# Low halves of the weight pieces of an encoder layer: a ScalarE copy with the sign turned and an accumulating DMA from GpSimd, where VectorE subtracted

## The chip, the cores and the metric

One core of a Trainium2 chip runs the whole kernel. The metric is device time in microseconds (us) of one execution, and the median of the runs is what is compared. A profile of one execution gives the trace; its span runs from the first to the last instruction, and the execution's own time is a little longer.

## The reference, cut to what matters

One layer of an encoder is applied to two request groups with the same weights: a prompt of 512 positions and a sample of 1024, both 1024 wide.

```python
h = _ln(x) * (1.0 + scale1) + shift1
proj = jnp.einsum('bld,de->ble', h, w_in)            # 1024 -> 4608
a = silu(_ln(_dwconv(a_val * sigmoid(a_gate))))      # 31 taps along positions
y_a = jnp.einsum('blc,cd->bld', a, conv_pw_w)
zb = x1 * _fftconv(v, filt[:, 0], hy_skip[0])        # long convolutions by FFT
zb = x2 * _fftconv(zb, filt[:, 1], hy_skip[1])
y_b = jnp.einsum('blc,cd->bld', zb, hy_out_w)
m = jax.nn.sigmoid(g_a) * y_a + jax.nn.sigmoid(g_b) * y_b
x = _ln(DEEPNORM_ALPHA * x + gate1 * (m @ w_out), ln1_g, ln1_b)
h = _ln(x) * (1.0 + scale2) + shift2
f = jnp.square(jax.nn.relu(h @ mlp_w1 + mlp_b1))     # 1024 -> 4096
x = _ln(DEEPNORM_ALPHA * x + gate2 * (f @ mlp_w2 + mlp_b2), ln2_g, ln2_b)
```

All of it is float32. The filters of the long convolutions come from a small MLP on the positions.

## The kernel before

A float32 product is made of three TensorE products of a shorter type, float32r: each operand is split into a high part (the value rounded to float32r) and a low part (the value minus its high part), and `mm3` adds high x high, high x low and low x high in PSUM. Activations are split where they are made. Weights come in **pieces** of 128 x 512 floats, 256 KB, 520 in all, and `wpiece_` makes each: SyncE's queue loads it into a `raw` buffer (4 of them); in 24 pieces near the end of each MLP VectorE multiplies a gate into `raw`; ScalarE copies `raw` to the high half of a `wt` buffer, which rounds it; VectorE subtracts that high half from `raw` into the low half. There are 6 `wt` buffers of two halves; 9 of the 520 pieces go into another pool, `pg`. `wpiece` raises the priority of these instructions.

The **main line** of work is, for the prompt group and the sample group in turn: `w_in` (72 pieces for each group, two at a time), `branches` (`w_y`, two at a time), `w_out_ln1` (four pieces serve a quarter of the columns), and `mlp`. The MLP runs in units of four hidden blocks. A unit multiplies the four hidden blocks with the left half of the columns of `mlp_w2` (four pieces, called phase D here), then with the right half (four other pieces, phase E); between units `mlp_up` makes the next hidden blocks with two pieces of `mlp_w1` each, the first of them before D. In D and E each of the four pieces is read in every block of 128 rows, so that all four are let go in the last block of the phase.

The **side line** is what the main line doesn't need at once: the filter MLP, the filters and their spectra (PSUM tiles `fx`), the 31-tap convolution (tiles `cv`, VectorE alone), the Hyena convolutions (FFT by matmuls). `pump` weaves it into the main line: a meter adds up an estimated cost of VectorE's and of TensorE's instructions, and side steps are taken while VectorE's sum is behind TensorE's. Each call of `self.V` is charged; calls through `self.nc.scalar` and `self.nc.gpsimd` are not.

The framework then orders each engine's instructions once more by priority and by its own estimate of when each is ready. Each engine executes its instructions in that order, and an instruction that waits holds all behind it on its engine. GpSimd (POOL) has little to do before: it clears tiles (`fp`, `cv`, `sg`) and issues the DMAs of the filter MLP's positions (`in_z_*`, 10 partitions, 40 KB, L617). Every VectorE instruction that goes through the meter, and every matmul, is shown at line L142.

Of the kernel before, what the change touches and what calls it, by code (L numbers as in the profile page):

```python
# [14 lines left out]
AF = mybir.ActivationFunctionType  # L15
ALU = mybir.AluOpType
# [142 lines left out]
class Enc:  # L159
# [50 lines left out]
    def wpiece_(self, src, shape, gate=None, w=None):  # L210
        raw = self.p_raw.tile(list(shape), F32, tag="raw", name="raw")
        self.nc.sync.dma_start(raw, src)
        if gate is not None:
            self.V.tensor_tensor(raw, raw, gate, op=ALU.mult)
        if w is None:
            w = self.p_wt.tile([128, 2] + list(shape[1:]), F32R, tag="wt", name="wt")
        self.split(raw, w[:, 0], w[:, 1])
        return w

    def mm3(self, ps, ah, al, bh, bl, first, last):  # L220
# [1159 lines left out]
```

## Time and profile before

| | us |
|---|---|
| median of 3 runs (2404.87 to 2413.45) | 2409.81 |
| the profiled execution | 2409.17 |
| its span | 2407.4 |
| TensorE (PE) busy in the span | 2339.7 |
| VectorE (DVE) busy | 1715.6 |
| ScalarE (ACT) busy | 859.7 |
| GpSimd (POOL) busy | 54.3 |

The profile page counts busy time by engine and shows it in 40 equal slices of the span. Other views list groups of equal instructions, who waited for whom, busy time in chosen stretches, the chain of work that ended last, and the instructions in order of time. Matmuls overlap, so that the mean duration of one is longer than its share of busy time.

### The profile page before, as it was taken

Reading aid. Unit: us, or ns where it says so; the run is one execution under the profiler, and the core shown is the slowest. Engines: PE = TensorE matmul, PEld = TensorE weight load, DVE = VectorE, ACT = ScalarE, POOL = GpSimd, SP = SyncE. Lnnn points to the kernel's source line nnn. Section 1 sums busy time; section 2 is a strip of 40 time slices with the busy share of each in tenths; the row PEclk is TensorE's granted clock in tenths of the full one; section 3 lists DMA queues with packets and bytes.
Section 4 is the critical chain, followed back from the end, with each engine's and each line's share of the span. In section 5 each row is a group of like instructions: output and inputs, shape, how many; then the busy total and the mean of one; then the engine's idle time right before and its main releaser. Section 6 shows DMA issues by size and latency. Waiting matters only on the chain.

```text
span 2407.4 us, 32989 instructions
## 1 busy us (share of the span) xinstructions
PE 2339.7 (97%) x12032; PEld 1947.7 (81%) x12032; DVE 1715.6 (71%) x3397; ACT 859.7 (36%) x1451; POOL 54.3 (2%) x149
## 2 busy tenths in 40 slices
PE   6999999999999999899999999999999999999997
PEld 3878777888888888888888887899888888888786
DVE  5988797877999989877988858749823433234567
ACT  3364422422222223465443352224742322322231
POOL 2110100000000000000000000000000000000000
PEclk9999999999999999999999999999999999999999
DMA  6555425663464566634433255544421111112231
GB/s 240 182 170 171 145 93 196 205 218 127 166 208 162 187 225 216 199 107 126 144 103 119 83 183 177 179 136 145 141 79 45 60 45 43 53 53 84 83 97 70
DMA packets 157864, 328.89 MB, mean 137 GB/s; under 512 B 18777, under 2 KB 27147, under 8 KB 157189
## 3 DMA queue, kind: packets, MB, share of 16 engines
q1 hardware_dynamic: 156869, 325.76, 41.1%
q8 instruction: 95, 1.56, 0.3%
q0 software_dynamic: 832, 1.02, 0.2%
q14 instruction: 68, 0.56, 0.1%
HBM read 265.04 MB, written 61.66 MB: 136 GB/s over the span
## 4 chain that ended last, share of the span: by engine, by line
PE 63%; DVE 9%; DMA 4%; issue 2%; ACT 1%; SPq 0%; DVEq 0%; ACTq 0%
PE mm L142 53%; PE fx L142 9%; DVE pg L142 3%; DVE fp L142 1%; DVE wt L142 1%; DMA sg<-ks 1%; PE tr L142 1%; DVE st L142 1%; DVE sg L142 1%; DVE sm L142 1%; DMA fp<-in_dec_s_dram 1%; DVE cv L142 1%; DMA pg<-d_grow 0%; DMA raw<-in_mlp_w_dram 0%; DMA sg<-in_ffn_w_dram 0%
## 5 line engine op out<-in xcount | busy, mean ns | idle before, releaser
L142 PE MATMUL mm<-pg,wt 128*128 128x512 f32 (+1 forms) x5544 | 1308.3, 391 | 4.1 <-DVE pg L142 3.3
L142 PEld LDWEIGHTS mm<-pg,wt 128*128 128x128 f32 x5544 | 1024.2, 189 | 219.5 <-issue 15.6
L142 PE MATMUL mm<-wt,pg 128*128 128x512 f32 (+1 forms) x3264 | 642.0, 355 | 7.2 <-DVE wt L142 3.8
L142 PEld LDWEIGHTS mm<-wt,pg 128*128 128x128 f32 x3264 | 537.3, 190 | 92.7 <-DVE wt L142 5.0
L199 ACT ACTIVATE wt<-raw 128x512 fp32r<-128x512 f32 x511 | 320.3, 630 | 743.7 <-PE mm L142 608.7
L142 DVE TENSOR_TENSOR wt<-raw,wt 128x512 fp32r<-128x512 f32 x511 | 346.3, 687 | 177.5 <-ACT wt L199 175.6
L142 DVE SCALAR_TENSOR_TENSOR cv<-cv,pp 128x512 f32<-128x512 f32 (+1 forms) x288 | 289.3, 1012 | 7.0 <-ACT cv L850 2.4
L142 DVE TENSOR_TENSOR pg<-so,pg 128x512 fp32r<-128x512 f32 (+1 forms) x219 | 135.4, 623 | 166.4 <-ACT so L1008 134.1
L142 DVE TENSOR_TENSOR pg<-pg,mm 128x512 f32<-128x512 f32 x168 | 113.6, 684 | 154.4 <-PE mm L142 154.3
L142 PEld LDWEIGHTS fx<-fp,fft 128*128 128x128 f32 x1536 | 177.5, 192 | 20.9 <-issue 14.2
L142 PE MATMUL fx<-fp,fft 128*128 128x128 f32 x1536 | 184.2, 277 | 2.1 <-DVE fp L142 1.0
L142 DVE TENSOR_TENSOR fp<-fp 128x256 f32<-128x256 f32 (+2 forms) x328 | 145.4, 483 | 16.2 <-ACT fp L377 10.8
L142 DVE TENSOR_TENSOR sg<-fx,sg 128x512 f32<-128x512 f32 (+1 forms) x162 | 98.8, 631 | 43.8 <-PE fx L142 29.5
L1006 ACT ACTIVATE so<-mm,pp 128x512 f32<-128x512 f32 (+1 forms) x99 | 66.4, 670 | 167.0 <-PE mm L142 167.0
L199 ACT ACTIVATE pg<-so 128x512 fp32r<-128x512 f32 (+1 forms) x120 | 64.7, 544 | 68.6 <-DVE so L142 51.9
L142 DVE TENSOR_TENSOR sg<-sg 128x256 f32<-128x256 f32 (+2 forms) x187 | 82.5, 461 | 5.2 <-ACT sg L887 3.9
L377 ACT ACTIVATE fp<-fx 128x512 f32<-128x512 f32 x48 | 28.7, 598 | 121.0 <-PE fx L142 110.7
L756 ACT ACTIVATE so<-mm 128x512 f32<-128x512 f32 x48 | 28.5, 593 | 95.3 <-PE mm L142 72.9
L1007 ACT ACTIVATE pg<-so 128x512 fp32r<-128x512 f32 (+1 forms) x99 | 61.0, 616 | 2.0
L1008 ACT ACTIVATE so<-so 128x512 f32<-128x512 f32 (+1 forms) x99 | 59.8, 604 | 0.0
L323 ACT ACTIVATE sg<-fx 128x512 f32<-128x512 f32 x48 | 28.7, 598 | 81.8 <-PE fx L142 75.8
L142 DVE TENSOR_TENSOR so<-mm,so 128x512 f32<-128x512 f32 x60 | 41.0, 685 | 20.2 <-PE mm L142 20.0
(115 smaller groups left out, 1485.0 us busy)
## 6 DMA issues: line engine op xcount, KB each, us to landing
raw<-in_mlp_w_dram SPq DMA_DIRECT2D x280, 256.0 KB
raw<-in_w_in_dram SPq DMA_DIRECT2D x144, 256.0 KB
fp<-in_w_ada_dram SPq DMA_DIRECT2D x48, 512.0 KB
raw<-in_w_out_dram SPq DMA_DIRECT2D x64, 256.0 KB
d_g<-so SPq DMA_DIRECT2D x48, 256.0 KB
ks<-sg SPq DMA_DIRECT2D x48, 256.0 KB
sg<-ks SPq DMA_DIRECT2D x48, 256.0 KB
so<-d_g SPq DMA_DIRECT2D x48, 256.0 KB
```

The lines of the kernel that those rows point to most:

```text
L142: return f(*args, **kw)
L199: self.nc.scalar.activation(hi, src, AF.Copy)
L323: nc.scalar.activation(kt, ps, AF.Copy)
L377: nc.scalar.activation(outs[-1][:, 4 * (pr % 2):4 * (pr % 2) + 4].rearrange("p (j w) c -> p j w c", j=2), ps, AF.Copy)
L756: nc.scalar.activation(o, ps, AF.Sigmoid)
L1006: nc.scalar.activation(r, ps[:, cols], AF.Relu, bias=self.pp[:, C_B1 + f:C_B1 + f + 1], scale=1.0)
L1007: nc.scalar.activation(p[:, 0, cols], r, AF.Square)
L1008: nc.scalar.activation(t, r, AF.Square)
```

## The change

The low half is no longer made by VectorE. ScalarE writes the piece twice: rounded into the high half, and rounded with the sign turned into the low half. Then GpSimd issues a DMA that adds the raw weights to the low half in place: from the weights' place in HBM, where 496 pieces are read a second time, or from `raw` in SBUF for the 24 gated ones. The sum is the same low part. The DMA's instruction waits for ScalarE; the matmuls that read the low half wait for the DMA to land. `split` stays as it is for the activations.

```diff
@@ -214,7 +214,9 @@
             self.V.tensor_tensor(raw, raw, gate, op=ALU.mult)
         if w is None:
             w = self.p_wt.tile([128, 2] + list(shape[1:]), F32R, tag="wt", name="wt")
-        self.split(raw, w[:, 0], w[:, 1])
+        self.nc.scalar.activation(w[:, 0], raw, AF.Copy)
+        self.nc.scalar.activation(w[:, 1], raw, AF.Copy, scale=-1.0)
+        self.nc.gpsimd.dma_start(w[:, 1], raw if gate is not None else src, accum_op=ALU.add)
         return w
```

The order moves at many places. On TensorE, where phase D of a unit of the sample's MLP ends and E begins (the last row of D, then E; `wt` numbers are the pieces, `mm` numbers the PSUM blocks), before:

```order
L142 MATMUL mm_19174<-wt_19073,pg2_18951 128x512 x3
L142 MATMUL mm_19208<-wt_19190,pg2_18433 128x512 x3
L142 MATMUL mm_19208<-wt_19195,pg2_18771 128x512 x3
L142 MATMUL mm_19208<-wt_19200,pg2_18845 128x512 x3
L142 MATMUL mm_19208<-wt_19205,pg2_18919 128x512 x3
L142 MATMUL mm_19222<-wt_19190,pg2_18433 128x512 x3
```

and the same place now:

```order
L142 MATMUL mm_19636<-wt_19534,pg2_19407 128x512 x3
L142 MATMUL mm_19674<-wt_19652,pg2_18875 128x512 x3
L142 MATMUL mm_19674<-wt_19658,pg2_19223 128x512 x3
L142 MATMUL mm_19674<-wt_19664,pg2_19299 128x512
L142 MATMUL mm_19688<-wt_19652,pg2_18875 128x512 x2
L142 MATMUL mm_19674<-wt_19664,pg2_19299 128x512 x2
L142 MATMUL mm_19674<-wt_19670,pg2_19375 128x512
L142 MATMUL mm_19688<-wt_19652,pg2_18875 128x512
L142 MATMUL mm_19688<-wt_19658,pg2_19223 128x512
L142 MATMUL mm_19674<-wt_19670,pg2_19375 128x512 x2
```

Before, the low half of the third piece was first read by the 8th matmul of E and that of the fourth by the 11th (the second of each three reads it); now these are the 10th and the 15th, since matmuls of the next block were drawn ahead.

On ScalarE, the copies for that same phase E and for the first pieces of the `mlp_up` that follows it, before:

```order
L199 ACTIVATE wt_19200<-raw_19198 128x512
L199 ACTIVATE wt_19205<-raw_19203 128x512
L199 ACTIVATE wt_19322<-raw_19320 128x512
L199 ACTIVATE wt_19327<-raw_19325 128x512
```

and now, L217 for the high half and L218 for the turned one:

```order
L217 ACTIVATE wt_19664<-raw_19662 128x512
L218 ACTIVATE wt_19664<-raw_19662 128x512
L217 ACTIVATE wt_19670<-raw_19668 128x512
L218 ACTIVATE wt_19670<-raw_19668 128x512
L217 ACTIVATE wt_19788<-raw_19786 128x512
```

The fourth piece of E now stands behind both copies of the third.

On TensorE, the end of the side line (`fx`, the last inverse FFT), before, in the prompt's MLP:

```order
L142 MATMUL mm<-pg,wt 128x512 x4
L142 MATMUL fx<-fft,sg 128x256 x8
L142 MATMUL mm<-pg,wt 128x512 x4
L142 MATMUL fx<-fft,sg 128x256 x4
L142 MATMUL mm<-pg,wt 128x512 x64
```

and now, in the prompt's `w_out`:

```order
L142 MATMUL mm<-wt,pg 128x256 x6
L142 MATMUL fx<-fft,sg 128x256 x8
L142 MATMUL mm<-wt,pg 128x256 x10
L142 MATMUL fx<-fft,sg 128x256 x4
L142 MATMUL mm<-wt,pg 128x256 x154
```

Before, 4256 matmuls of the main line stood ahead of this last `fx` row, now 3014: the meter no longer charges VectorE for the pieces, and the side line is woven in earlier.

## Rows read from the trace of the kernel before

**Rows 1.** The page: busy time by engine; 40 slices in tenths, three engines

```profile
PE 2339.7 (97%) x12032; PEld 1947.7 (81%) x12032; DVE 1715.6 (71%) x3397; ACT 859.7 (36%) x1451; POOL 54.3 (2%) x149
...
PE   6999999999999999899999999999999999999997
...
DVE  5988797877999989877988858749823433234567
```

**Rows 2.** Waits of TensorE for VectorE: us in total, times, longest us

```profile
PE fx L142 <- DVE sg L142: 7.1, 12, 1.1
PE mm L142 <- DVE pg L142: 6.7, 3, 3.3
PE mm L142 <- DVE wt L142: 3.8, 5, 1.4
PE fx L142 <- DVE fp L142: 2.4, 4, 0.7
```

**Rows 3.** The page's groups: the copies and subtractions of the pieces; busy us, mean ns

```profile
L199 ACT ACTIVATE wt<-raw 128x512 fp32r<-128x512 f32 x511 | 320.3, 630 | 743.7 <-PE mm L142 608.7
L142 DVE TENSOR_TENSOR wt<-raw,wt 128x512 fp32r<-128x512 f32 x511 | 346.3, 687 | 177.5 <-ACT wt L199 175.6
```

**Rows 4.** The chain, in order of time: start us, us; the sample's MLP in steady flow

```profile
1738.61 474.04 PE mm L142 x2091
```

**Rows 5.** Timeline: phase D starts at 1920.75; its end; start us, us

```profile
1920.75 39.60 PE L142 MATMUL mm<-wt,pg 128*128 128x512 f32 x174
...
1940.67 2.67 ACT L199 ACTIVATE wt<-raw 128x512 fp32r<-128x512 f32 x4 [17.47 <-PE mm L142]
1941.33 2.05 DVE L142 TENSOR_TENSOR wt<-raw,wt 128x512 fp32r<-128x512 f32 x3 [0.66 <-ACT wt L199]
```

**Rows 6.** GpSimd's own DMAs, L617, 40 KB: durations on POOL in ns; time to landing

```profile
L617 POOL DMA_DIRECT2D fp<-in_z_s_dram x17: 521/521/521, 4.8 to 317.6; - x17
...
DMA to landing us min/median/max: 2.2/3.0/6.1
```

**Rows 7.** Timeline: the first piece's load is issued, and ScalarE's copy that waited for it

```profile
4.19 0.59 SPq L212 DMA_DIRECT2D raw<-in_w_in_dram  x1
...
7.62 0.63 ACT L199 ACTIVATE wt<-raw 128x512 fp32r<-128x512 f32 x1 [4.55 <-DMA raw<-in_w_in_dram]
```

**Rows 8.** The page's DMA queues: packets, MB, share of 16 engines

```profile
q1 hardware_dynamic: 156869, 325.76, 41.1%
```

**Rows 9.** Timeline: `w_out` of the prompt, copies of four pieces of a quarter

```profile
981.83 2.79 ACT L199 ACTIVATE wt<-raw 128x512 fp32r<-128x512 f32 x4 [3.15 <-PE mm L142]
...
988.88 2.79 ACT L199 ACTIVATE wt<-raw 128x512 fp32r<-128x512 f32 x4 [4.26 <-PE mm L142]
```

**Rows 10.** Timeline: TensorE's gap at the prompt's last unit

```profile
1475.11 6.43 PE L142 MATMUL mm<-wt,pg 128*128 128x512 f32 x15 [3.03 <-DVE pg L142]
```

**Rows 11.** Stretches: us, busy us (count) of PE, PEld, DVE, ACT, POOL; PEclk; DMA share; GB/s

```profile
1475.00:1480.00 5.00, 4.89 (x12) 3.88 (x13) 4.87 (x9) 2.19 (x5) 0.00 (x0) 0.50 0.88 250
1480.00:1485.00 5.00, 5.00 (x21) 4.11 (x20) 1.58 (x3) 0.00 (x0) 0.00 (x0) 0.90 1.03 384
...
2230.00:2235.00 5.00, 5.00 (x20) 4.00 (x19) 5.00 (x7) 0.00 (x0) 0.00 (x0) 0.81 0.73 279
```

**Rows 12.** Stretches, the same columns: with the side line, `w_in` late, after it

```profile
0.00:1374.00 1374.00, 1328.81 (x7223) 1100.03 (x7224) 1166.10 (x2390) 518.06 (x870) 54.28 (x149) 1.00 0.50 166
...
840.00:960.00 120.00, 116.79 (x676) 100.42 (x675) 109.13 (x226) 39.56 (x65) 0.68 (x6) 1.00 0.68 224
...
1800.00:2200.00 400.00, 400.00 (x1766) 331.32 (x1765) 130.94 (x188) 112.84 (x188) 0.00 (x0) 1.00 0.16 49
```

**Rows 13.** Waits of GpSimd: us in total, times, longest us

```profile
POOL cv L795 <- PE fx L142: 277.2, 6, 177.4
POOL sg L326 <- DMA kny<-sg: 222.3, 10, 114.4
```

**Rows 14.** The chain: the longest stretch that a piece's load held

```profile
802.00 5.76 DMA raw<-in_w_in_dram
```

## The prediction

> **What bounds the kernel now.** I read busy time first. TensorE is busy for 2339.7 of 2407.4 us, in nearly every slice; VectorE is close to it for the first two thirds only, and then falls to between a quarter and a half [rows 1]. So taking 346.3 us of subtractions from VectorE [rows 3] can give back only what TensorE waits for VectorE. The waits say how much that is: 7.1 + 6.7 + 3.8 + 2.4 = 20.0 us in the four largest entries, of which just 3.8 us are the subtractions themselves [rows 2]. That is the whole prize, 0.8% of the time. In the sample's MLP there is none: 2091 matmuls follow each other in 474.04 us, 226.7 ns each [rows 4], and TensorE is busy for 400 of 400 us [rows 12].
>
> What can be lost is decided where a weight buffer is refilled just in time. With two pieces in use and six buffers (`w_in`, `w_y`, `mlp_up`), two further pairs are ready: 24 matmuls for each pair and group block are 5.4 us, and a refill has at least two such times. With four pieces in use (`w_out`, phases D and E), only two of the next four can be ready; the third and fourth go into buffers that are let go in the last block of the phase. Those I call **handoffs**. Every unit of the MLP has one, D to E: 7 in the prompt, 8 in the sample. `w_out` has 8 in each group, one for each quarter of each pass. That makes 31.
>
> **The handoff in the MLP.** The rows of one [rows 5]: D starts at 1920.75, its 96 matmuls of 226.7 ns end at 1942.5. ScalarE starts the four freed copies at 1940.67, VectorE the subtractions at 1941.33, 0.69 us each. The third piece's low half is made by 1942.0, and was first read by the 8th matmul of E, at 1942.5 + 7 x 0.2267 = 1944.1. So before there were 2 us to spare, and TensorE shows no gap.
>
> Now ScalarE makes two copies for each piece, 0.63 us each [rows 3]. The third piece's turned copy ends near 1940.67 + 1.28 = 1941.95; its low half is read by the 10th matmul, at 1942.5 + 9 x 0.2267 = 1944.55: 2.6 us are left for the DMA. The fourth stands behind it on ScalarE: ready at 1943.25, read by the 15th matmul at 1945.7, so 2.4 us are left. Whatever the DMA takes beyond 2.4 us, from its issue to the matmul that it releases, TensorE stands still, and nothing covers it: the side line now ends before the prompt's MLP. What queues behind the waiting instruction on GpSimd there are the next pieces' DMAs alone, which have a whole phase.
>
> **How long the DMA takes.** No row shows an accumulating transfer. GpSimd's own DMAs of 40 KB take 2.2 us at least, 3.0 in the median and 6.1 at most to land, 0.52 us of that on POOL [rows 6]. A 256 KB piece loaded by SyncE was used 7.62 - 4.19 = 3.4 us after its issue [rows 7]. The queue's packets hold 0.411 x 2407.4 x 16 / 156869 = 0.101 us of an engine for 2 KB [rows 8]; a piece has 8 of them on each engine, 0.8 us. An accumulating DMA must also read its destination, so I add a second 0.8 us: 3.4 + 0.8 = 4.2 us. The ends are 2.2 and 6.1 us; I take 4.2 because the nearest row in size is the 3.4.
>
> The Trainium skill (DMA: Bandwidth & Descriptors, Anatomy of one DMA — SWDGE (gpsimd) path) fits a GpSimd DMA by 2.0 us plus bytes over 436 GB/s. By that a piece is estimated at 2.6 us and hardly any handoff would stand still: that is the third rival below. The trace doesn't agree for small transfers: the fit makes 2.1 us of 40 KB, and the median here is 3.0 [rows 6]. The skill (Collectives: The Full Stack, The bandwidth ceiling) also says that an adding DMA reads two sources, so that its read side carries twice the traffic; no run here shows it so far.
>
> **The sum**, on the profiled execution's 2409.2 us (the median of the runs is 2409.8, so nothing is shifted):
>
> - MLP handoffs: 15 x (4.2 - 2.4) = 27 us.
> - `w_out` of the sample: a quarter ends with matmuls of 256 columns, a little over half as long. The third piece's buffer is free 2.1 us before the quarter's end and needed 1.7 us after; less 0.2 us until ScalarE starts and 1.28 us of copies, and with the fourth again behind the third on ScalarE, 2.0 us are left. 8 x 2.2 = 18 us.
> - `w_out` of the prompt: the four copies of a quarter recur after 988.88 - 981.83 = 7.05 us there, 2.79 us of ScalarE [rows 9]; now they are 5.0 us beside the layer norm's own. I add 0.3 us for each: 8 x 2.5 = 20 us. It may partly lie in gaps that the layer norm leaves already.
> - The last units: there the gated pieces come late, and TensorE already has a gap of 3.03 us behind VectorE's work on them [rows 10]. A copy and the DMA replace the subtraction, 0.63 + 4.2 - 0.69 = 4.1 us, in both groups: 8 us.
> - The clock: after the gap of 3.03 us the granted clock was 0.50, the 1.2 GHz level, for the next 5 us and 0.90 for 5 more, with 12 and 21 matmuls where 226.7 ns each would let in 22, so that 11 matmuls or 2.5 us were lost; after another gap, of 3.3 us [rows 2], it was 0.81 for one such stretch, with 20 of them [rows 11]. My gaps are mostly near 2 us, for which I have no row: between 0 and 2.5 us each, taken as 0.5, 31 x 0.5 = 15 us.
> - VectorE's relief: between 0 and 20 us back; half, -10 us. The side line is woven in earlier, so that VectorE has the same mixture in less time: the meter drops 0.6 us for each piece, and the 944 matmuls of 512 and 298 of 256 columns that now come after the side line are 249 us in which there is nothing left to relieve.
> - ScalarE's 520 added copies, 328 us in all, lie beside other work elsewhere: with them it is busy for about half of the span. If that cover fails it is at the handoffs, where they are counted.
>
> 2409.2 + 27 + 18 + 20 + 8 + 15 - 10 = **2487 us**, 3.2% slower. With 6.1 us for the DMA and 2.5 us of clock for each handoff it is 2409 + 56 + 33 + 35 + 12 + 78 = 2623; with 2.2 us and all of the relief 2409 + 0 + 6 + 4 - 20 = 2399.
>
> **The rivals.** *DMA engines become the bound* while the side line runs. Its first 1374 us hold 0.50 x 1374 = 687 us of full DMA work, and `w_in` late is at 0.68 [rows 12]. The stretch shrinks to about 1125 us; the 104 pieces that leave it take 84 us along, and some 170 pieces stay. With two reads, 1.6 us each, that is 603 + 272 = 875 us of 1125, 78%: crowded, not full. It decides from (1125 - 603) / 170 = 3.1 us of all engines for a piece, about four times a plain copy. At 4 us the stretch takes 1283 us: 158 us more, about 2650. For it: a load already held the chain for 5.76 us in there [rows 14]; and the DMAs now stand on GpSimd among clears that waited up to 177 us at once [rows 13], though the planner set them in the order in which it holds them ready.
>
> *The DMA is hidden and VectorE's relief shows*: it decides below 2.4 us, near the shortest of GpSimd's transfers, 2.2 us [rows 6]; 2395 to 2399 us, faster. Against it is that the 40 KB median is already 3.0.
>
> *No change*: at 2.6 us the handoffs cost 3 + 5 + 7 us, the ends 5, and the relief gives 20 back: 2409 us.
>
> **How the numbers follow.** The handoffs at about my price, 2430 to 2570: 0.53. The engines or GpSimd's queue as the bound, from 2570 up: 0.25. Hidden and faster: 0.13. No change: 0.09. A difference of 0.3%, 7 us, is about what a measurement of this kernel can tell from none. So faster has 0.13, the same 0.09, slower 0.78. The range is 2400 to 2640: below it lies most of the faster case, above it about half of the engines' case.
>
> **What would show it.** VectorE near 1370 us; ScalarE near 1190. POOL's DMAs of `wt` landing in about 4 us in the sample's MLP. TensorE with a gap of about 2 us at each D to E there, released by the DMA of `wt`, and full flow between. The last `fx` near 1130 us plus what the first part lost. I am wrong if transfers land in under 2.5 us (no gaps, faster), or if TensorE's gaps lie in `w_in` and name DMAs of the side line or clears on GpSimd.

## The result and the profile after

The changed kernel takes 2735.61 us in the median (2727.41 to 2742.91, 4 runs), beside 2409.81 us for the kernel before on the same chip: a ratio of 1.1353, 95% interval 1.1297 to 1.1409, 13.5% slower. 2487 had been predicted, with a range up to 2640. The direction was right; the loss is 326 us where 77 were priced. A fourth run of the kernel before took 3927.58 us and is left out here; the expectations below count 324 us, from a median with that run in it.

The page of the changed kernel first: busy time by engine, three rows of the 40 slices, and the DMA queues (packets, MB, share of 16 engines).

```profile
PE 2463.0 (90%) x12032; PEld 2027.9 (74%) x12032; DVE 1412.5 (52%) x2877; ACT 1122.3 (41%) x1977; POOL 505.8 (18%) x669
...
PE   6899989999999988786799898997899999999997
...
PEclk9999999999999999887899998998999999999999
DMA  8989676756886568557678687875775444444663
...
q1 hardware_dynamic: 156869, 325.76, 36.4%
q0 software_dynamic: 75712, 137.36, 29.9%
```

VectorE's subtractions are gone: it is busy for 1412.5 us, before for 1715.6 [rows 1]. TensorE does the same 12032 matmuls, but two things grew: it stands idle for 2740.8 - 2463.0 = 277.8 us, before 67.7, and it is busy for 123.3 us longer with the same work. That second part is nearly all the clock, below its full level in the slices where TensorE had gaps, around the middle above all: the mean granted clock is 0.948 for 0.994 before, and 2339.7 x (0.994 / 0.948 - 1) is 114 us. GpSimd's queue carries 75712 packets, before only 832. Each holds an engine for 0.299 x 2740.8 x 16 / 75712 = 0.173 us, where a packet of SyncE's queue holds one for 0.102, much as before [rows 8].

TensorE's waits in the changed kernel (us in total, times, longest), to be read against [rows 2]:

```profile
PE mm L142 <- DMA wt<-in_mlp_w_dram: 64.2, 28, 5.2
PE mm L142 <- DMA wt<-in_w_out_dram: 53.0, 28, 4.4
PE fx L142 <- DVE sg L142: 27.6, 18, 3.3
PE fx L142 <- DVE fp L142: 18.4, 11, 7.7
```

The two new entries at the top are accumulating DMAs of `w_out`, whose pieces are used four at a time, and of the MLP, whose `mlp_w2` pieces are (the view doesn't part them from those of `mlp_w1`). The waits for VectorE did not fall with VectorE's load; they rose, from 7.1 and 2.4 us to 27.6 and 18.4.

The DMAs' own line, L219: duration on POOL in ns (min/median/max), then the time from issue to landing.

```profile
L219 POOL DMA_DIRECT2D wt<-in_mlp_w_dram x256: 862/862/1682, 1272.3 to 2693.4; - x128
...
DMA to landing us min/median/max: 3.2/6.2/12.9
```

One handoff of the sample's MLP, from phase D to E, in the timeline of the changed kernel (start us, us; in brackets the idle time before and what ended it), which answers to [rows 5]:

```profile
2231.82 12.85 PE L142 MATMUL mm<-wt,pg 128*128 128x512 f32 x56
...
2240.63 0.63 ACT L217 ACTIVATE wt<-raw 128x512 fp32r<-128x512 f32 x1 [16.95 <-PE mm L142]
2241.16 0.61 ACT L218 ACTIVATE wt<-raw 128x512 fp32r<-128x512 f32 x1
2241.69 0.62 ACT L217 ACTIVATE wt<-raw 128x512 fp32r<-128x512 f32 x1
...
2242.07 0.86 POOL L219 DMA_DIRECT2D wt<-in_mlp_w_dram  x1 [17.24 <-PE mm L142]
...
2243.11 0.86 POOL L219 DMA_DIRECT2D wt<-in_mlp_w_dram  x1 [0.18 <-issue]
...
2246.59 1.43 PE L142 MATMUL mm<-wt,pg 128*128 128x512 f32 x5 [1.92 <-DMA wt<-in_mlp_w_dram]
...
2248.95 7.42 PE L142 MATMUL mm<-wt,pg 128*128 128x512 f32 x25 [0.93 <-DMA wt<-in_mlp_w_dram]
```

It goes as the prediction drew it: ScalarE's two copies of the third piece, then of the fourth, a DMA behind each; and TensorE stops for both, where the prediction had hardly anything left for the fourth. The third piece's DMA is issued at 2242.07 and releases a matmul at 2246.59, 4.5 us; the fourth's takes 2248.95 - 2243.11 = 5.8 us. The gaps are 1.92 and 0.93 us. The chain of waits shows this place as one entry, and one like it at `w_out` of the sample, at 1870 us (start us, us, what held the chain):

```profile
1870.40 7.12 DMA wt<-in_w_out_dram
...
2243.11 5.79 DMA wt<-in_mlp_w_dram
```

Among the longest entries of the chain there are 7 such for pieces of `w_out` of the sample and 8 for pieces of its MLP, 3.3 to 9.5 us long, 5.85 in the mean.

What the clock is after the gaps, in stretches behind that handoff (columns as in [rows 11]):

```profile
2248.00:2249.00 1.00, 0.07 (x2) 0.06 (x1) 0.00 (x0) 0.00 (x0) 0.00 (x0) 0.81 0.98 291
2249.00:2250.00 1.00, 1.00 (x3) 0.82 (x4) 0.00 (x0) 0.00 (x0) 0.00 (x0) 0.50 1.08 258
...
2251.00:2252.00 1.00, 1.00 (x4) 0.81 (x3) 0.00 (x0) 0.00 (x0) 0.00 (x0) 0.50 1.12 205
2252.00:2253.00 1.00, 1.00 (x5) 0.76 (x5) 0.03 (x1) 0.00 (x0) 0.00 (x0) 0.98 0.31 53
2250.00:2255.00 5.00, 5.00 (x19) 4.04 (x18) 1.38 (x2) 0.00 (x0) 0.00 (x0) 0.80 0.51 95
```

After its gaps of 1.92 and 0.93 us, with 1.43 us of matmuls between them, TensorE flows again from 2248.95, but the granted clock is 0.50, the 1.2 GHz level, until 2252. Between 2250 and 2255 it starts 19 matmuls where 22 fit at 226.7 ns each. The DMA engines are full from the gap until then: the four accumulating DMAs and four loads that this handoff sets off come as one burst, though the mean share of this MLP is 0.51.

### The profile page after: what moved, and what is told of

It is laid out like the page before. It is cut to its first block, busy times and chain, and to the rows that moved or that the text cites. A ratio compares the mean times of both kernels' runs of the same rounds, so it can differ in the third digit from the quotient of the medians.

```text
span 2740.8 us, 34055 instructions
## 1 busy us (share of the span) xinstructions
PE 2463.0 (90%) x12032; PEld 2027.9 (74%) x12032; DVE 1412.5 (52%) x2877; ACT 1122.3 (41%) x1977; POOL 505.8 (18%) x669
## 3 DMA queue, kind: packets, MB, share of 16 engines
q0 software_dynamic: 75712, 137.36, 29.9%
## 5 line engine op out<-in xcount | busy, mean ns | idle before, releaser
L142 PE MATMUL mm<-pg,wt 128*128 128x512 f32 (+1 forms) x5544 | 1330.1, 395 | 19.3 <-DMA wt<-in_mlp_w_dram 4.3
L142 PE MATMUL mm<-wt,pg 128*128 128x512 f32 (+1 forms) x3264 | 715.9, 380 | 131.7 <-DMA wt<-in_mlp_w_dram 59.9
L142 PEld LDWEIGHTS mm<-wt,pg 128*128 128x128 f32 x3264 | 586.8, 209 | 244.6 <-DMA wt<-in_mlp_w_dram 73.5
L217 ACT ACTIVATE wt<-raw 128x512 fp32r<-128x512 f32 x511 | 315.1, 625 | 800.6 <-PE mm L142 644.2
L219 POOL DMA_DIRECT2D wt<-in_mlp_w_dram x256 | 222.2, 920 | 859.7 <-ACT wt L218 432.1
L218 ACT ACTIVATE wt<-raw 128x512 fp32r<-128x512 f32 x511 | 310.1, 617 | 0.0
L142 DVE SCALAR_TENSOR_TENSOR cv<-cv,pp 128x1024 f32<-128x1024 f32 (+1 forms) x288 | 288.3, 1015 | 24.0 <-ACT cv L802 13.3
L219 POOL DMA_DIRECT2D wt<-in_w_in_dram x144 | 127.1, 897 | 568.1 <-ACT wt L218 496.7
L142 PEld LDWEIGHTS fx<-fp,fft 128*128 128x128 f32 x1536 | 189.0, 201 | 47.1 <-issue 38.5
L142 DVE TENSOR_TENSOR fp<-fp 128x256 f32<-128x256 f32 (+2 forms) x328 | 145.6, 486 | 23.2 <-ACT fp L816 12.0
L219 POOL DMA_DIRECT2D wt<-in_w_out_dram x64 | 55.6, 924 | 265.9 <-ACT wt L218 139.6
L199 ACT ACTIVATE pg<-so 128x512 fp32r<-128x512 f32 (+1 forms) x120 | 64.3, 543 | 77.7 <-DVE so L142 62.5
L142 DVE TENSOR_TENSOR sg<-sg 128x256 f32<-128x256 f32 (+2 forms) x187 | 82.6, 463 | 13.5 <-ACT sg L889 11.9
L142 PE MATMUL fx<-fp 128*128 128x256 f32 (+1 forms) x132 | 38.3, 371 | 33.0 <-DMA fp<-d_w 15.7
```

Source lines behind the costliest of these rows:

```text
L142: return f(*args, **kw)
L199: self.nc.scalar.activation(hi, src, AF.Copy)
L217: self.nc.scalar.activation(w[:, 0], raw, AF.Copy)
L218: self.nc.scalar.activation(w[:, 1], raw, AF.Copy, scale=-1.0)
L219: self.nc.gpsimd.dma_start(w[:, 1], raw if gate is not None else src, accum_op=ALU.add)
```

## The experiments

Three theories stood at first. A: the handoffs, with a DMA that lands later than priced, and the clock after each. B: the transfers crowd the DMA engines everywhere, in proportion to their number. C: the order, since the meter no longer charges VectorE for the pieces and the side line is woven in earlier. The table gives what each run measured (ratio to the kernel before on the same chip; span, TensorE's busy time and the rest of the span from its profile).

| run | median us | ratio (95%) | span | PE busy | PE idle |
|---|---|---|---|---|---|
| before | 2409.81 | | 2407.4 | 2339.7 | 67.7 |
| changed | 2735.61 | 1.1353 (1.1297-1.1409) | 2740.8 | 2463.0 | 277.8 |
| e1_pairs | 2557.77 | 1.0626 (1.0602-1.0651) | 2545.4 | 2382.7 | 162.7 |
| e2_fours | 2624.49 | 1.0887 (1.0842-1.0931) | 2616.1 | 2408.6 | 207.5 |
| e3_unmetered | 2527.55 | 1.0489 (1.0474-1.0505) | 2525.8 | 2380.2 | 145.6 |
| e4_metered | 2721.12 | 1.1297 (1.1273-1.1321) | 2720.6 | 2444.7 | 275.9 |
| e5_nodma | 2472.63 | 1.0265 (1.0250-1.0280) | 2470.6 | 2357.3 | 113.3 |
| e6_plain_pool | 2589.71 | 1.0755 (1.0735-1.0776) | 2584.8 | 2398.1 | 186.7 |
| e8_from_raw | 2687.31 | 1.1156 (1.1137-1.1174) | 2686.8 | 2435.9 | 250.9 |
| e9e_buf8 | 2609.11 | 1.0831 (1.0807-1.0854) | 2601.4 | 2389.7 | 211.7 |
| e11_nodma_metered | 2399.15 | 0.9965 (0.9954-0.9976) | 2397.1 | 2330.9 | 66.2 |
| e12_win_metered | 2454.51 | 1.0191 (1.0170-1.0211) | 2456.2 | 2354.2 | 102.0 |
| e13_buf8_metered | 2546.28 | 1.0573 (1.0548-1.0598) | 2537.5 | 2374.2 | 163.3 |
| e14_before_buf8 | 2414.16 | 1.0037 (1.0022-1.0052) | 2410.9 | 2337.4 | 73.5 |
| e15_pool_sub | 2533.22 | 1.0521 (1.0500-1.0542) | 2530.0 | 2380.1 | 149.9 |
| e16_pool_win | 2462.56 | 1.0224 (1.0201-1.0246) | 2460.4 | 2355.5 | 104.9 |

### Which pieces cost

The condition under which the new lines run; the other pieces are split as before:

```diff
+        if shape[1:] == (4, 128):        # e1_pairs; != in e2_fours
+            ... the two copies and the DMA ...
+        else:
+            self.split(raw, w[:, 0], w[:, 1])
```

> The accumulating DMA only for the pieces that are used two at a time (w_in, w_y, mlp_w1: 304 of 520); w_out and mlp_w2, used four at a time, keep VectorE's subtraction. Theory A (handoffs: the 31 places where the third and fourth of four pieces go into buffers that have just come free wait for a DMA of 6.2 us, and the clock falls after each): these waits go, what stays is what the first 1000 us lose, some 50 us: 2430 to 2480. Theory B (the transfers crowd the DMA engines everywhere, in proportion to their number): 304/520 of the 324 us lost stay, about 2600. Theory C (the side line is woven in earlier because the meter no longer charges VectorE, and that is what costs): most of the loss stays, 2600 to 2700, since the w_in pieces, which shift it most, are still uncharged.

> The complement: the accumulating DMA only for w_out and mlp_w2 (216 of 520 pieces). Theory A: the handoffs' loss stays whole, 2640 to 2690. Theory B: 216/520 of 324 us, about 2545. Theory C: the w_in pieces are charged to the meter again, so the side line lies nearly as before: 2430 to 2500.

Both expectations count the pieces wrong: GpSimd's queue shows 46912 packets in e1_pairs and 29632 in e2_fours, 832 of them as before, which at 144 a piece are 320 and 200 pieces, not 304 and 216. B's times by these counts would be about 2609 and 2534.

The four-at-a-time pieces alone cost 2624.49 - 2409.4 = 215 us. That is short of A's 2640, and far above B's 2534 and C's 2500. The two-at-a-time pieces cost 148 us, a time that no theory had in its range: more than A gives, less than B and C. Their run also shifts the side line nearly as far as the change does: the last `fx` matmul stands behind 3256 matmuls of `mm` blocks, before behind 4272, in the changed kernel behind 3030; in e2_fours it is 3993. So A holds, and something else stands beside it. The landing of the DMAs in e2_fours:

```profile
DMA to landing us min/median/max: 3.3/5.6/12.8
```

The sample's MLP, where no side line is left and only handoffs and the late gated pieces at the end can cost, shows A alone. One stretch from the first pieces of that MLP to the end, in the kernels before, e2_fours and changed (columns as in [rows 12]):

```profile
1714.90:2407.40 692.50, 675.74 (x2984) 556.83 (x2983) 299.23 (x502) 215.01 (x368) 0.00 (x0) 0.99 0.21 68
```

```profile
1864.70:2616.10 751.40, 700.67 (x3003) 569.99 (x3001) 256.30 (x441) 249.86 (x441) 57.93 (x67) 0.97 0.35 87
```

```profile
1986.20:2740.80 754.60, 703.71 (x3016) 571.65 (x3014) 211.37 (x366) 285.68 (x515) 121.46 (x140) 0.97 0.51 114
```

Idle time is 16.8, 50.7 and 50.9 us: the changed kernel loses no more there than e2_fours, although it makes twice the pieces by GpSimd's DMAs (140 for 67) and its DMA share is 0.51 for 0.35. In this stage the loss is that of the four-at-a-time pieces; the other transfers beside them add nothing that shows.

### The order of the side line

```diff
-        self.split(raw, w[:, 0], w[:, 1])
+        self.nc.scalar.activation(w[:, 0], raw, AF.Copy)
+        self.nc.vector.tensor_tensor(w[:, 1], raw, w[:, 0].bitcast(F32), op=ALU.subtract)
```

> The kernel before, with VectorE's subtraction of the pieces issued past the meter: no DMA, no second copy, only the order's shift of the side line. Theories A and B: within 1% of before, 2400 to 2435, if anything slower since VectorE has its old work in a shorter stretch. Theory C: most of the loss, 2600 or more.

```diff
         self.nc.gpsimd.dma_start(w[:, 1], raw if gate is not None else src, accum_op=ALU.add)
+        self.V.us += 0.6 / SHARE
```

> The changed kernel, with 0.6 us charged to VectorE's meter for each piece as the subtraction was: the side line is spread as before, DMA and second copy stay. Theory A: about as the changed kernel in the MLP and w_out, 2680 to 2750. Theory B: the 1374 us that the side line had before are less crowded, 2600 to 2680. Theory C: most of the loss goes, below 2500.

Both answers surprised. The shift of the side line alone, with VectorE's work whole, costs 118 us, so C is real, if smaller than its 2600, and A's 1% was wrong. Yet the charge restored in the changed kernel brings back just 14 us, to a time in A's range. To see the shift with VectorE relieved, I took away the DMA, and then also restored the charge:

```diff
-        self.nc.gpsimd.dma_start(w[:, 1], raw if gate is not None else src, accum_op=ALU.add)
+        self.V.us += 0.6 / SHARE         # in e11_nodma_metered alone
```

> The changed kernel without its DMA: ScalarE's two copies and the order of the side line stay, the low halves are left as the rounded weights with the sign turned, so the output isn't the reference's and the time is that of the kernel without the addition. Theory A (the wait for the landing at the handoffs is the cost, some 210 us by the run with only the four-at-a-time pieces): all waits for wt DMAs go, what stays is what the earlier side line costs with VectorE relieved, between 0 and the 118 us that the shift alone cost: 2410 to 2530. Theory D (ScalarE's second copies hold the handoffs): 2600 or more.

> As the run without the DMA (two copies by ScalarE, nothing added, the output isn't the reference's), but with 0.6 us charged to VectorE's meter for each piece, so that the last inverse FFT stands behind 4274 matmuls of the main line again, as it did before (4272), for 3030 in the changed kernel. If the 64 us left there were the earlier side line: 2395 to 2415. If they were ScalarE's second copies: about 2470 again.

e5_nodma loses 64 us and e11_nodma_metered gains 9. They differ in the one line that charges the meter. So VectorE's relief, less whatever ScalarE's second copies cost, is worth 9 us, and the earlier side line costs 73 us beside it. Most of that lies in one place, 960 to 1200 us, here before, e5_nodma and e11_nodma_metered:

```profile
960.00:1200.00 240.00, 228.91 (x1389) 200.55 (x1389) 196.14 (x490) 128.58 (x227) 0.54 (x8) 0.98 0.45 144
```

```profile
960.00:1200.00 240.00, 195.48 (x1276) 177.85 (x1276) 216.38 (x554) 103.50 (x180) 0.93 (x14) 0.91 0.47 150
```

```profile
960.00:1200.00 240.00, 233.40 (x1429) 204.66 (x1428) 165.67 (x434) 167.06 (x311) 0.80 (x12) 1.00 0.45 146
```

TensorE is idle there for 44.5 us without the charge and 6.6 with it, a difference of 37.9 us of 47.1 in the whole span. VectorE executes 554 instructions there without the charge and 434 with it, none of them a subtraction of a piece: the side line's steps are packed closer. What TensorE waits for in e5_nodma in that stretch:

```profile
PE tr L142 <- ACT pg L513: 14.7, 2, 14.1
PE fx L142 <- DVE fp L142: 11.4, 2, 7.6
PE mm L142 <- DVE pg L142: 8.8, 5, 2.9
```

Of the 44.5 us, 26.1 lie before the last `fx` matmul ends at 1155.9 us, and 18.4 behind it. Before it, TensorE, ScalarE and VectorE wait for one another in turn, in Fourier steps (`fx`) and in main-line matmuls that need `pg`; I read this as too little of the main line between the packed steps. Behind it there is no side line left to fill a gap: one wait of 14.1 us is that of the layer norm's transposes (`tr`) for ScalarE, at the end of `w_out`, where e11_nodma_metered has 1.4 us at most. No run tries these two by themselves.

### Why the DMA lands late

```diff
-        self.nc.gpsimd.dma_start(w[:, 1], raw if gate is not None else src, accum_op=ALU.add)
+        self.nc.gpsimd.dma_start(w[:, 1], raw if gate is not None else src)   # e6_plain_pool
+        self.nc.gpsimd.dma_start(w[:, 1], raw, accum_op=ALU.add)              # e8_from_raw
```

> The changed kernel with the same DMA from GpSimd, but a plain copy that overwrites the low half, nothing added (the output isn't the reference's). If the reading of the destination makes the landing late (twice the engine time: 0.173 us for each packet against 0.102), the landing falls from 6.2 to some 4.5 us and the handoffs' waits by a third: 2620 to 2680. If GpSimd's path itself (the issue, the writing of descriptors, the queue) makes it late, landing stays near 6 us and the time near 2720.

> The changed kernel with all pieces added from raw in SBUF, as the gated ones are, so that no weight is read from HBM a second time. If the second read from HBM makes the landing late, the landing falls to the 4.5 to 5.4 us that the gated pieces' rows show, and the time to 2620 to 2690; if not, the time stays within 1% of 2735, or rises, since raw (4 buffers) is held until the DMA has landed and the next loads start later.

Line, queue and landing of e6_plain_pool:

```profile
L219 POOL DMA_DIRECT2D wt<-in_mlp_w_dram x256: 527/527/548, 1208.8 to 2537.4; - x128
...
DMA to landing us min/median/max: 2.3/4.1/9.3
```

```profile
q0 software_dynamic: 75712, 137.36, 17.9%
```

Landing and queue of e8_from_raw:

```profile
DMA to landing us min/median/max: 3.2/4.4/12.3
```

```profile
q0 software_dynamic: 75712, 137.36, 30.3%
```

The same DMA without the addition lands in 4.1 us, its issue takes 0.53 us of POOL for 0.86, and a packet holds an engine for 0.179 x 2584.8 x 16 / 75712 = 0.098 us for 0.173. It saves 146 of the 326 us, more than expected. So the adding, with the load that it puts on the engines, costs 0.33 us at the issue, 0.075 us a packet and 2.1 us of landing. The source matters less for the engines: from SBUF a packet holds 0.172 us just the same, though the landing falls to 4.4 us, so that the engine time of the packets alone doesn't set the landing. That gives back only 48 us. SyncE's loads of `raw` now wait for these DMAs to land, 476 times and 1582 us in all; in the changed kernel they wait for ScalarE's copies, 370 times and 1240 us. I take the held `raw` to be what eats up the gain, which was not tried by itself; this run's time lies in its expected range, but by my reading not only for the reason expected.

### Buffers: taking the handoffs away

```diff
-            self.p_raw = P("raw", 4)
-            self.p_wt = P("wt", 6)
+            self.p_raw = P("raw", 3)
+            self.p_wt = P("wt", 8)
-                self.p_fp = P("fp", 11, early)
+                self.p_fp = P("fp", 10, early)
```

e9e_buf8 has this in the changed kernel, e13_buf8_metered has the charge of the meter besides, e14_before_buf8 has it in the kernel before.

> The changed kernel with 8 wt buffers for 6 (raw 3 for 4, fp 10 for 11, to make room), so that all four pieces of the next phase lie in buffers that are free a phase earlier. Theory A: the handoffs' waits for wt DMAs go, with the clock they cost, some 200 us: 2520 to 2580, near the run with only the two-at-a-time pieces. Theory B (crowded DMA engines) or D (ScalarE): the same pieces, bytes and copies at the same rate, so 2690 or more.

> The kernel before with 8 wt buffers (raw 3, fp 10): what the pools' sizes do by themselves. If the gain of 126 us with 8 buffers came from the handoffs, which had 2 us to spare before the change, there is nothing to gain here: 2400 to 2420. If the pools relieve something else, it gets faster here too, 2380 or less.

> The changed kernel with 8 wt buffers (raw 3, fp 10) and the meter charged. If the three causes add (handoffs some 210 us, order 64, load in w_in 48), this has the load and a rest of the handoffs in w_out and the prompt's MLP, 2490 to 2550. If the order costs nothing beside the others, as charging the meter alone gave only 14 us back, 2590 to 2610.

With 8 buffers 126 us come back, and the same pools give the kernel before nothing (0.4% slower). TensorE's waits for piece DMAs in e9e_buf8:

```profile
PE mm L142 <- DMA wt<-in_w_out_dram: 19.2, 12, 3.2
...
PE mm L142 <- DMA wt<-in_mlp_w_dram: 3.6, 6, 1.5
```

The MLP's 64.2 us have shrunk to 3.6; those of `w_out`, where a quarter lasts 7 us and the DMA nearly as long, are still 19.2. That is part of why the time stayed above the expected 2580; the rest was not separated. With the meter charged as well it is 2546, in the upper part of the range for causes that add.

### The load beside the side line

```diff
+        if src.tensor.name == 'in_w_in_dram':
+            ... the two copies and the DMA ...
+            self.V.us += 0.6 / SHARE
+        else:
+            self.split(raw, w[:, 0], w[:, 1])
```

> The accumulating DMA for the 144 w_in pieces alone, charged to the meter as the subtraction was; all others as before. Two pieces are in use there, so there are no handoffs, and the order is nearly that of before: what is left is VectorE's relief against the DMA engines' load beside the side line. Relief: 2395 to 2405. Crowding, by the difference of 48 us in the w_in stages between the run with the meter charged and the run with only the four-at-a-time pieces: 2450 to 2465. Earlier readings of the time in w_in of the changed kernel as an effect of the order alone: 2405 to 2415.

2454.51, as the crowding said: 47 us lost where there are no handoffs and the order is nearly the old one, and 55 beside e11_nodma_metered, which has VectorE's relief. Two stretches of `w_in` without the DMA (e11_nodma_metered), then with it (e12_win_metered):

```profile
0.00:250.00 250.00, 228.12 (x1038) 177.42 (x1038) 165.21 (x333) 153.85 (x266) 36.58 (x59) 0.99 0.60 195
250.00:820.00 570.00, 560.11 (x3015) 453.32 (x3014) 465.92 (x835) 205.39 (x349) 15.81 (x68) 1.00 0.51 173
```

```profile
0.00:250.00 250.00, 214.50 (x939) 161.55 (x940) 154.56 (x313) 142.05 (x244) 92.46 (x123) 0.97 0.90 243
250.00:820.00 570.00, 545.68 (x2846) 436.09 (x2845) 435.83 (x783) 204.15 (x350) 80.10 (x137) 0.99 0.70 197
```

The DMA engines go from 0.60 to 0.90 busy in the first 250 us and from 0.51 to 0.70 after that, and TensorE starts 99 and 169 matmuls fewer. Its waits in e12_win_metered are small and of many kinds:

```profile
PE fx L142 <- DVE fp L142: 14.1, 14, 2.1
PE fx L142 <- DVE sg L142: 12.7, 14, 3.3
PE tr L142 <- DMA fp<-in_w_ada_dram: 8.8, 9, 3.1
...
PE mm L142 <- DMA wt<-in_w_in_dram: 5.8, 3, 4.4
```

Only 5.8 us are for the pieces themselves. `w_ada`, a load of the side line, is waited for 8.8 us, in e11_nodma_metered 2.8. I read the rest too as the side line's own loads coming later in a fuller queue; how much of the two VectorE entries goes back to late loads was not separated. Two other causes do not show: no wait of TensorE in the first 860 us names a clear on GpSimd, and VectorE's instructions are no longer than before (`fp<-fp` of 128 x 512 takes 683 ns in the mean in both).

Three kernels without the charge part the DMA further. Up to the same matmul, the last of `w_in` or near it, there is no DMA (e5_nodma), the plain one (e6_plain_pool) and the accumulating one (the changed kernel); TensorE's order is the same in the last two, and differs at 32 places in the first:

```profile
0.00:858.40 858.40, 820.52 (x4293) 656.63 (x4294) 670.70 (x1279) 376.79 (x635) 52.95 (x131) 1.00 0.54 180
```

```profile
0.00:872.50 872.50, 823.48 (x4293) 658.56 (x4294) 671.82 (x1279) 376.20 (x635) 127.63 (x271) 0.99 0.67 219
```

```profile
0.00:908.90 908.90, 834.82 (x4292) 666.10 (x4293) 671.94 (x1279) 376.02 (x635) 174.99 (x271) 0.98 0.75 210
```

The plain DMA costs 14 us there and the accumulating one 50, with the same number of instructions on GpSimd (271) in both and VectorE equally busy in all three. So most of the loss in `w_in` comes with the adding: its longer issue, engine time and landing, which these runs do not part.

### GpSimd's own subtraction

```diff
+        self.nc.scalar.activation(w[:, 0], raw, AF.Copy)
+        self.nc.gpsimd.tensor_tensor(w[:, 1], raw, w[:, 0].bitcast(F32), op=ALU.subtract)
+        self.V.us += 0.6 / SHARE         # e16_pool_win: for w_in alone, VectorE for the others
```

> The subtraction of every piece on GpSimd as one instruction, reading raw and the high half, in place of the second copy and the DMA; the meter is charged as before. If only the DMA (its landing and its load) was the loss, this keeps VectorE relieved with neither: 2395 to 2405, faster than both kernels, as long as GpSimd's instruction is under the 2 us to spare at the handoffs. If GpSimd's instruction is several us long or holds VectorE up, the handoffs wait for it: 2450 or more.

> GpSimd subtracts for the 144 w_in pieces alone, where two pieces are in use and VectorE is nearly full; VectorE subtracts for the others; the meter is charged as before. There are no handoffs there, so a long instruction on GpSimd is hidden: 2398 to 2408 by VectorE's relief alone; if GpSimd's reads hold VectorE up, 2415 or more and longer VectorE instructions in w_in.

Neither beats the kernel before: they lose 125 and 54 us. Both fall in the range set for a GpSimd instruction that holds others up. In e15_pool_sub TensorE waits for GpSimd's low halves for 15.2 us, in 16 places. GpSimd's instruction in e16_pool_win (busy us, mean ns, idle before), and two groups of VectorE's over the first 860 us, there and in the kernel before:

```profile
L219 POOL TENSOR_TENSOR wt<-raw,wt 128x512 fp32r<-128x512 f32 x144 | 221.4, 1541 | 450.8 <-ACT wt L217 421.6 <-issue 19.9 <-DMA fp<-in_dec_p_dram 9.1
```

```profile
L142 DVE TENSOR_TENSOR sg<-fx,sg 128x512 f32<-128x512 f32 x64 | 42.3, 681 | 21.4 <-PE fx L142 18.2 <-DMA sg<-ks 3.3
...
L142 DVE TENSOR_TENSOR fp<-fp 128x512 f32<-128x512 f32 x44 | 34.2, 817 | 0.1
```

```profile
L142 DVE TENSOR_TENSOR sg<-fx,sg 128x512 f32<-128x512 f32 x64 | 42.4, 682 | 11.9 <-PE fx L142 10.0 <-DMA sg<-ks 1.6
L142 DVE TENSOR_TENSOR fp<-fp 128x512 f32<-128x512 f32 x56 | 35.5, 683 | 0.0
```

The group with both operands in SBUF (`fp`) takes 817 ns for 683, the one with an operand in PSUM (`fx`) 681 for 682. Most of the relief is paid back in this way: over the first 860 us VectorE's 1154 instructions in e16_pool_win keep it busy for 708.2 us, the 1154 of e12_win_metered for 625.6, and the subtractions taken from it there were 99.6 us. How the remaining loss comes about was not separated. The Trainium skill (SBUF — State Buffer, Who interferes with whom) says that a VectorE instruction with two SBUF inputs contends with a GpSimd instruction that reads SBUF; the trace agrees, at 134 ns in the mean for that group.

## Why the prediction was wrong, step by step

The sum failed at four of its terms: the DMA's 4.2 us and the clock's 0.5 us at a handoff were too small, the side line's shift stood in it as a part of a gain, and the load beside the side line stood at nothing. With the first two at their upper ends the prediction had 2623 us; the rest, up to 2736, comes from the other two.

**The bound and the prize: right.** TensorE was the bound, and removing VectorE's subtractions is worth 9 us by e11_nodma_metered, second copies included, where half of 20 had been taken. VectorE came to 1412.5 us for 1370, ScalarE to 1122.3 for 1190.

**The handoff: the mechanism right, the DMA's time too small.** The place, the two pieces, the order of copies on ScalarE and a gap of about 2 us behind the third piece came as drawn; the fourth added 0.93 us in the handoff shown. The step that failed is the 4.2 us for the DMA, made of a SyncE load (3.4) and a second read (0.8). As engine time the second read was sized right: 144 packets a piece in GpSimd's queue are 9 on each engine, and 0.075 us more for each is 0.7 us. But a plain DMA from GpSimd already took 4.1 us in the median among the other transfers, not 3.4, and adding made it 6.2: 2.1 us more, of which 0.33 are the issue and 0.7 engine time, the rest not separated. In e2_fours the median is 5.6. Put into the prediction's own terms, 5.6 gives 15 x 3.2 = 48, 8 x 3.6 = 29 and 8 x 3.9 = 31 for `w_out`, and 2 x 5.5 = 11 for the ends: 119 us, where 4.2 gave 73. The idle time of e2_fours rose by 207.5 - 67.7 = 139.8 us, so the DMA's time makes up most of the excess, not all of it. In the sample's MLP alone the terms give 8 x 3.2 + 5.5 = 31 us, and the idle time rose by 50.7 - 16.8 = 33.9. The 6.1 us that was taken as the upper end is near the middle of what the DMAs took; their longest is 12.9. The value came from the nearest row in size, a transfer on another queue at the start of the kernel.

**The clock: mis-sized by more than four.** 0.5 us for each handoff was taken from between 0 and 2.5, 15 us in all. In e2_fours TensorE is busy 2408.6 - 2339.7 = 68.9 us longer with the same matmuls, 2.2 us a handoff, within the bounds of 0 and 2.5. That the two upper ends together gave 2623 us in the prediction and e2_fours took 2624 is partly luck, since neither stands at its end.

**The earlier side line: the wrong sign.** The prediction saw that the meter would weave it in earlier, and let it cut the relief to half, 10 us, and no further: VectorE was to have "the same mixture in less time". It costs 64 us with the relief counted (e5_nodma) and 118 without (e3_unmetered). The meter's charge for the pieces was also what kept the side line apart, as e5_nodma and e11_nodma_metered show. What decides there is not the engine's sum of work: by the trace of e5_nodma the packed steps wait for each other, and behind them nothing is left to fill the waits of `w_out` and its layer norm.

**The crowding: the right load, a wrong rule.** 1.6 us of all engines for a piece was foreseen (9 packets on each engine by 0.173), and "crowded, not full" as well, but a cost was set only from the point at which the engines are full. 47 us are lost at 0.70 to 0.90 busy (e12_win_metered). Of the rival's other half, clears held up on GpSimd's queue, TensorE's waits in the changed kernel show one of 3.2 us. One of the prediction's signs of being wrong came in part: TensorE has gaps in `w_in` that name a load of the side line, `w_ada`, 10.0 us for 2.4 before.

**The sum.** Handoffs with the clock 215 (e2_fours), the order 64 (e5_nodma), the load in `w_in` 47 (e12_win_metered): 326 us, and the changed kernel loses 326. This agreement is partly luck, since the parts are not independent. With the side line back in its old place (e4_metered) the handoffs and the load would make 262 us, and 312 were lost; the other 50 lie for the most part in the prompt's MLP, where the side line is again: between the same main-line matmuls e4_metered takes 571 us there (from 1117 us on), e2_fours 528 (from 1057 on). The DMAs of `mlp_w1`, which e2_fours leaves to VectorE, would explain it; that was not tried by itself. By this reading restoring the meter alone helps so little because the side line meets DMAs in its old place, and is packed too close in its new one.

**The figures cited from pages.** The Trainium skill's fit for a GpSimd DMA (DMA: Bandwidth & Descriptors, Anatomy of one DMA — SWDGE (gpsimd) path), an estimate of 2.6 us for a piece, lies between the fastest plain one (2.3 us) and the median (4.1) of e6_plain_pool, and below the fastest accumulating one (3.2). That an add has two sources to read, as the Trainium skill says of the reduce step of a collective (Collectives: The Full Stack, The bandwidth ceiling), agrees with the packets: 0.173 us for 0.098, 1.8 times.

## What to carry to other kernels

Work moved from a busy engine to a DMA is paid at the place where a buffer is refilled just in time: price the transfer by how long it takes among the others of its burst, and count the clock after every gap. Where a meter or a cost table sets the order, an operation removed from it moves everything behind it; keep the charge, or the run measures two changes. Ask first what TensorE waits for the relieved engine at all: here it was 20 us in the largest entries, and none of the kernels tried that make the low halves elsewhere (by DMA, with more buffers too, or on GpSimd) got any of it.

## What the runs showed of the hardware

- An accumulating DMA of 256 KB from GpSimd: 0.86 us of POOL to issue (plain: 0.53), 3.2/6.2/12.9 us to land in the changed kernel (min/median/max; plain, in e6_plain_pool: 2.3/4.1/9.3), 0.173 us an engine for a packet (plain: 0.098). From SBUF 4.4 us in the median, with the same 0.172 us a packet.
- Idle time of TensorE is followed by slow busy time: 68.9 us beside 139.8 us of added idle time in e2_fours, 123.3 beside 210.1 in the changed kernel, 40.5 beside 77.9 in e3_unmetered. Over the runs with 30 us or more of added idle time, each microsecond of it came with 0.35 (e9e_buf8) to 0.59 us (the changed kernel) of slower work.
- A GpSimd subtraction of 128 x 512 with both operands in SBUF takes 1.54 us, and while it does so for the pieces of `w_in`, a group of VectorE's instructions of that size with two SBUF operands goes from 683 to 817 ns in the mean, and one with an operand in PSUM stays at 681.
